# Low parts of the gate and up weights by adding transfers from HBM instead of VectorE subtractions

## The chip, the cores and the metric

The kernel runs on one core of a Trainium2 chip. A core has five engines with an instruction queue each: TensorE (PE in the profile, with its weight loads as PEld), VectorE (DVE), ScalarE (ACT), GpSimd (POOL) and SyncE (SP), and 16 DMA engines that move data between HBM and the on-chip memory. An engine works through its queue in order and waits for the others at semaphores. The metric is the device time of one execution in microseconds; of several runs the median is taken.

## The reference

A small decoder trunk on 512 tokens of width 1024: one short-convolution layer, then one sliding-window attention layer, each followed by a SwiGLU feed-forward block. All is float32.

```python
def swiglu(h, w_gate_up, w_down):
    g, u = jnp.split(h @ w_gate_up, 2, axis=-1)
    return (jax.nn.silu(g) * u) @ w_down

h = x
for l in range(DEPTH):                      
    if l < N_A:                             
        mix = short_conv_mixer(rmsnorm(h, a_pre_norm[l]), a_w_in[l], a_conv_w[l], a_w_out[l])
        h = h + rmsnorm(mix, a_post_norm[l])
    else:                                   
...
        h = h + rmsnorm(attn, b_post_norm[j])
    ff = swiglu(rmsnorm(h, ffn_pre_norm[l]), ffn_w_gate_up[l], ffn_w_down[l])
    h = h + rmsnorm(ff, ffn_post_norm[l])
return h
```

With D_FF = 2816 the gate and up projections have 22 column blocks of 128 each, in each of the two layers.

## The kernel before

**Two parts for each number.** TensorE multiplies in the type float32r, which holds fewer bits than float32. So every operand is kept as a rounded high part and the remainder, the low part. `mm3` (lines 167 to 170) multiplies with three matmuls: high weight by low activation (L168), high by high (L169), low weight by high activation (L170). In `project` the weights are the stationary operand: 8 blocks of 128 rows times three matmuls of 128x512 make 24 matmuls for one piece of weights, which is a 128x1024 tile of 512 KB and gives 128 output columns for all 512 tokens.

**How a piece is prepared.** `split_weights` (L150) takes four steps, on three engines:

- `fetch` (L132 to 138): SP issues a transfer of 512 KB from HBM into a buffer `raw`; the pool `wraw` has N_RAW = 6 of them. The next fetch into a buffer waits until its last reader is done.
- L161, L162: a pair `whi`, `wlo` is taken from the pool `wsp`, which has N_W = 5 of each. A pair comes free when TensorE has done with it.
- L163: ScalarE copies `raw` into `whi`, which rounds it (`AF.Copy`, no factor).
- L164: VectorE subtracts `whi` from `raw` into `wlo`.

`Ahead` (L317) does the same in two separate calls, L333 and L338, for the first three blocks of gate and up weights of a layer, written into an order by hand. `split_weights` with `slots=True` keeps its parts elsewhere (L157, L158).

**The feed-forward block.** `ffn` works in ROUNDS of blocks f: 0 to 5, 6 to 13, 14 to 21. For each f the gate piece and the up piece are prepared and projected (L731 to L737), and `gate_pair` or `gate` turns the two results into an activation: a sigmoid on ScalarE (L608 in `gate_pair`), multiplications on VectorE, rounding and remainder again. f = 0, 1 and 2 come from `Ahead`; f = 3 to 21 come from `split_weights`, 19 blocks with two pieces in each of the two layers, 76 pieces.

After the first two rounds `seven` multiplies that round's activations with the down weights by a scheme of seven products instead of eight. It uses the same five pairs `whi`, `wlo` (L669, L670) and the same six raw buffers, three jobs ahead (SEVEN_LEAD). One of its jobs is 12 matmuls, or 6 where it covers one block only, so that pairs come free there faster than in the projections. After the last round `first_half` and `second_half` multiply with the down weights directly and finish the layer.

**Order of the work.** Within a `tc.manual_schedule` block the instructions stand in each engine's queue as written. The projections of f = 3 to 21, the gates and `seven` are outside such blocks: there a scheduler picks the order at build time by its own estimates, and places the semaphore waits. At run time each engine keeps to that order.

GpSimd issues no transfer in this kernel. In the feed-forward blocks it only takes the power that ends a norm (L266, L286), at their end.

Of the kernel before, what the change touches and what calls it, by code (L numbers as in the profile page):

```python
# [10 lines left out]
F32 = mybir.dt.float32  # L11
F32R = mybir.dt.float32r
AF = mybir.ActivationFunctionType
ALU = mybir.AluOpType
# [41 lines left out]
def yoco_kernel(  # L56
# [20 lines left out]
    nc = tc.nc  # L77
# [14 lines left out]
    def name(s):  # L92
        uid[0] += 1
        return f"{s}_{uid[0]}"

    def slot(s, dt=F32, w=S):
        return big.tile([P, w], dt, tag="slot", name=name(s), padded_shape=[P, S])
# [10 lines left out]
    def bank(s, pool=None):  # L108

        if pool is None:  # L110
            pool = (ps_mm, ps_sc, ps_mm, ps_pt)[turn[0] % 4]
            turn[0] += 1
        return pool.tile([P, S], F32, tag="bank", name=name(s))
# [14 lines left out]
    def g(col, k):  # L128
        return gt[:, col + k : col + k + 1]


    def fetch(src, n=D):  # L132
        raw = wraw.tile([P, D], F32, tag="raw", name=name("raw"))
        dst = raw[:, :n]
        if len(src.shape) == 3:
            src, dst = src.rearrange("k p c -> p k c"), dst.rearrange("p (k c) -> p k c", c=S)
        nc.sync.dma_start(dst, src)
        return raw
# [8 lines left out]
            h = at[1].start // S  # L147
            return self.of[h][:, at[1].start - h * S : at[1].stop - h * S]

    def split_weights(src, raw=None, slots=False):  # L150
        if raw is None:
            raw = fetch(src)
        if slots:
            hi, lo = Two("whi", F32R), Two("wlo", F32R)
            for h in range(2):
                c = slice(h * S, (h + 1) * S)
                nc.scalar.activation(hi[:, c], raw[:, c], AF.Copy)  # L157
                nc.vector.tensor_tensor(out=lo[:, c], in0=raw[:, c], in1=hi[:, c].bitcast(F32),  # L158
                                        op=ALU.subtract)
            return hi, lo  # L160
        hi = wsp.tile([P, D], F32R, tag="whi", name=name("whi"))  # L161
        lo = wsp.tile([P, D], F32R, tag="wlo", name=name("wlo"))  # L162
        nc.scalar.activation(hi, raw, AF.Copy)  # L163
        nc.vector.tensor_tensor(out=lo, in0=raw, in1=hi.bitcast(F32), op=ALU.subtract)  # L164
        return hi, lo

    def mm3(out, whi, wlo, xhi, xlo, start, stop, **kw):
# [4 lines left out]
    def project(ps, w, x, c0=0, c1=S):  # L172

        whi, wlo = w
        for k in range(KT):
            kk = slice(k * P, (k + 1) * P)
            mm3(ps[:, c0:c1], whi[:, kk], wlo[:, kk], x[k][0][:, c0:c1], x[k][1][:, c0:c1],
                k == 0, k == KT - 1)
# [185 lines left out]
    with tc.manual_schedule(engines=ALL):  # L364
# [6 lines left out]
        for k in range(KT):  # L371
            hi, lo = xs[k]
            nc.scalar.activation(hi, xt[k], AF.Copy, scale=g(G_APRE, k))
            nc.vector.scalar_tensor_tensor(
                out=lo, in0=xt[k], scalar=g(G_APRE, k), in1=hi.bitcast(F32),
                op0=ALU.mult, op1=ALU.subtract,
            )
            for k0, k1 in CUTS:
                if k == max(k0 - 1, 0):
                    kk = slice(k0 * P, k1 * P)  # L380
                    for t in range(3):
                        hi, lo = ws[t]
                        nc.scalar.activation(hi[:, kk], first[t][:, kk], AF.Copy)
                        nc.vector.tensor_tensor(
                            out=lo[:, kk], in0=first[t][:, kk], in1=hi[:, kk].bitcast(F32),
                            op=ALU.subtract,
# [35 lines left out]
    for f in range(KT):  # L422
        if f < 2:
            pc, pu, pb = begun[f]
        else:
# [12 lines left out]
            out=t, in0=cu, scalar1=g(G_CONV, 16 + f), scalar2=None, op0=ALU.mult  # L438
        )
        for lag, tap in ((1, 1), (2, 0)):  # L440
            nc.vector.scalar_tensor_tensor(
                out=t[:, lag:], in0=cu[:, : S - lag], scalar=g(G_CONV, 8 * tap + f),
                in1=t[:, lag:], op0=ALU.mult, op1=ALU.add,
# [4 lines left out]
        hi, lo = slot("yhi", F32R), slot("ylo", F32R)  # L448
# [5 lines left out]
    def first_half(load, x, n, take, ws1=None):  # L454

        ws = [load(0, j) for j in range(n // 2)]
        raws = [fetch(load(1, j, True)) for j in range(min(2, n // 2))]
        ws1 = []

        def more():  # L460
            if len(ws1) < n // 2:
                ws1.append(split_weights(None, raws.pop(0), True))
                j = len(ws1) + len(raws)
                if j < n // 2:
                    raws.append(fetch(load(1, j, True)))

        with tc.manual_schedule(engines=ALL):
            pss = [bank("pmix") for _ in range(2)]
            for t in range(2):
                unit(pss[t], t, ws, x, range(n - 2), n)  # L470
                more()
            for t in range(2):
                unit(pss[t], t, ws, x, range(n - 2, n), n)
                take(t, 0, pss[t])
            for t in (2, 3):
                ps = bank("pmix")
                unit(ps, t, ws, x, range(n), n)
                more()
                take(t, 0, ps)
        return ws1  # L480
# [23 lines left out]
    def second_half(ws, x, n, res, ahead):  # L504

        k0 = n - 2
        for t in range(NB):
            ps = bank("pmix", ps_mm)
            if t == NB - 1:
                unit(ps, t, ws, x, range(k0), n)  # L510
                for b in range(4):
                    res.turn(b, (0, 1))
                unit(ps, t, ws, x, range(k0, n), n)
                for f in range(4):
                    res.split(0, f, 0)
            else:
                unit(ps, t, ws, x, range(n), n)
            if t == 0:
                ahead.one()
                ahead.one()  # L520
            res.take(t, 1, ps)
            if t < NB - 1:
                tile_done(res, t, ahead)
# [41 lines left out]
    def first_weights(l):  # L565
        return [w_gu[l, f, j] for f in range(3) for j in range(2)]
# [13 lines left out]
    ahead = Ahead(first_weights(0))  # L580
# [4 lines left out]
    def ffn(l, before, ahead, gain, gpres, following):  # L585
# [143 lines left out]
        for rd, (f0, f1) in enumerate(ROUNDS):  # L729
            final = rd == len(ROUNDS) - 1  # L730
            for f in range(2 if rd == 0 else f0, f1):  # L731
                pss = []
                for j in range(2):
                    w = ahead.ready[4 + j] if f == 2 else split_weights(w_gu[l, f, j])
                    pss.append(bank("pgu", (ps_sc, ps_pt)[j] if f == 2 else None))
                    project(pss[-1], w, xs)
                (gate if final else gate_pair)(*pss)  # L737
            n = f1 - f0
            if not final:
                seven(range(f0 // 2, f1 // 2), acts, rd == 0)  # L740
                acts = []
                continue

            def load(half, j, raw=False):
                src = w_dn[l, f0 // 2 + j, half : 4 - half : 3 - 2 * half]
                return src if raw else split_weights(src)

            res = Update(mix, gain, gpres, True)
            res.load()

            def take_last(t, half, ps):
                res.take(t, half, ps)
                res.scale(t, half)

            ws1 = first_half(load, acts, n, take_last)
            if gpres:
                ahead = Ahead(following)
                with tc.manual_schedule(engines=ALL):
                    second_half(ws1, acts, n, res, ahead)
                return res, ahead  # L760
            with tc.manual_schedule(engines=ALL):
                for t in range(NB):
                    if t < NB - 1:
                        ps = bank("pmix")
                        unit(ps, t, ws1, acts, range(n), n)
                        res.take(t, 1, ps)
                        res.mean(t)
                    else:
                        for c in (0, 256):
                            ps = bank("pmix")  # L770
                            unit(ps[:, :256], t, ws1, acts, range(n), n, 0, c, c + 256)
                            res.take_quarter(t, c, ps)
                    res.scale(t, 1)
                    for c in range(0, D, D if t < NB - 1 else S):
                        e = c + (D if t < NB - 1 else S)
                        res.update(t, c, e)
                        (nc.sync if c == 0 else nc.scalar).dma_start(out[t, :, c:e],
                                                                     hs[t][:, c:e])

    res, ahead = ffn(0, res, ahead, B_FFN[0], [G_KV, G_BPRE], [  # L780
        w_k[0], w_k[1], w_v[:, 0:D], w_v[:, D:], w_q[0], w_q[1]])
    xkv, xq = res.x
# [203 lines left out]
    with tc.manual_schedule(engines=ALL):  # L986
# [45 lines left out]
        src = [p.rearrange("p (h d) -> p h d", d=HD) for p in pv]  # L1032
        for j in range(NB):
            nc.scalar.activation(dst[j][0], src[j], AF.Copy)
        for j in range(NB):
            nc.vector.tensor_tensor(out=dst[j][1], in0=src[j], in1=dst[j][0].bitcast(F32),
                                    op=ALU.subtract)

    with tc.manual_schedule(engines=ALL):
        for i in range(KT + 2):  # L1040
            for c in ORDER.split():
# [5 lines left out]
                op, n = c[0], [int(d) for d in c[1:].rstrip("-")]  # L1047
                t = i - late
                if op == "g":

                    u = 2 * (t - EARLY - 1) + n[0]
                    if u in (-2, -1, 2, 3):
                        j = u + 2 if u < 0 else u
# [8 lines left out]
                elif op == "G":  # L1062
                    t += LEAD + 1
                    of = qs
                    if KT <= t < KT + 4:
                        j = t - KT
# [9 lines left out]
        ahead = Ahead(first_weights(1))  # L1076
# [10 lines left out]
        for t in range(NB):  # L1087
# [17 lines left out]
            if t < NB - 1:  # L1105
                tile_done(res, t)
    ffn(1, res, ahead, B_FFN[1], [], [])


# [85 lines left out]
```

## Time and profile before

| | |
|---|---|
| time, median of 3 runs | 1075.13 us (1073.75 to 1075.42) |
| the profiled execution | 1075.27 us |
| its span, first to last instruction | 1073.5 us |
| granted TensorE clock | 0.998 |
| HBM read, written | 103.46 MB, 2.10 MB |

The span is 1.8 us below the time of its execution. Busy time is what an engine spent in instructions, with waits left out. In the rows of instruction groups the line of kernel.py comes first, then engine, operation, output and inputs by their names, the count, the total busy time and the mean of one in ns; behind the second bar stands how long the engine was idle before them, and what ended most of that. The profile's chain is followed back from the last instruction, at each step to what released it.

### The profile page before, as it was taken

To read this page: it belongs to the slowest core of one execution; us is meant where nothing else is said; L and a number is where in the kernel's file an instruction comes from. 1 tells how busy PE (TensorE), PEld (TensorE's weight loads), DVE (VectorE), ACT (ScalarE), POOL (GpSimd) and SP (SyncE) were. 2 spreads that over 40 slices of the span, in tenths; PEclk is the share of its full clock that TensorE was granted. 3 is DMA by queue.
4 is the path that set the end of the run, shared out by engine and by line. 5 is a ranking of instruction groups with operands and counts; after the bars stand their busy time and mean duration, and the time that the engine had idled before them with its cause. 6 is when DMAs were issued, how large, how long until landed. Compare 5 with 4: busy or idle time off the path is not lost.

```text
span 1073.5 us, 13531 instructions
## 1 busy us (share of the span) xinstructions
PE 1060.8 (99%) x5268; PEld 894.0 (83%) x5268; DVE 656.5 (61%) x1069; ACT 444.6 (41%) x787; POOL 91.7 (9%) x90
## 2 busy tenths in 40 slices
PE   9899999999999999999999999999999999999997
PEld 7788888988888888888898888889888888888886
DVE  6665654376644784444568998666674568634344
ACT  6222234454433343223474777655353334322221
POOL 2421100000000000000021532020000000000001
PEclk9999999999999999999999999999999999999999
DMA  8433242030733044324212122302135221622201
GB/s 318 159 117 99 87 141 87 21 108 6 240 99 98 20 138 156 98 99 137 79 43 76 40 80 79 113 26 72 56 125 178 86 74 40 198 98 98 98 1 79
DMA packets 36864, 106.43 MB, mean 99 GB/s; under 512 B 3776, under 2 KB 4672, under 8 KB 36800
## 3 DMA queue, kind: packets, MB, share of 16 engines
q1 hardware_dynamic: 36224, 104.91, 30.3%
q8 instruction: 41, 0.67, 0.3%
q10 hardware_dynamic: 576, 0.66, 0.2%
q14 instruction: 23, 0.19, 0.1%
HBM read 103.46 MB, written 2.10 MB: 98 GB/s over the span
## 4 chain that ended last, share of the span: by engine, by line
PE 93%; DVE 3%; issue 1%; ACT 1%; POOL 1%; DMA 0%; POOLq 0%; DVEq 0%; SPq 0%; ACTq 0%
PE pgu L168 15%; PE pgu L169 15%; PE pgu L170 15%; PE pmix L169 4%; PE pmix L168 4%; PE pmix L170 4%; PE px L170 2%; PE px L169 2%; PE px L168 2%; PE pcub L392 2%; PE pz L170 1%; PE pz L169 1%; PE pz L168 1%; PE psc L867 1%; PE pq L168 1%
## 5 line engine op out<-in xcount | busy, mean ns | idle before, releaser
L168 PE MATMUL pgu<-xlo,whi 128*128 128x512 f32 (+1 forms) x768 | 285.6, 372 | 1.0 <-DVE xlo L312 1.0
L169 PE MATMUL pgu<-xhi,whi 128*128 128x512 f32 (+1 forms) x768 | 285.2, 371 | 0.0
L170 PE MATMUL pgu<-xhi,wlo 128*128 128x512 f32 (+1 forms) x768 | 285.1, 371 | 0.0
L163 ACT ACTIVATE whi<-raw 128x1024 fp32r<-128x1024 f32 x117 | 123.4, 1060 | 299.1 <-issue 159.4
L164 DVE TENSOR_TENSOR wlo<-raw,whi 128x1024 fp32r<-128x1024 f32 x117 | 156.1, 1335 | 123.2 <-ACT whi L163 123.2
L168 PEld LDWEIGHTS pgu<-xlo,whi 128*128 128x128 f32 x768 | 144.7, 188 | 26.4 <-DVE xlo L312 1.4
L169 PEld LDWEIGHTS pgu<-xhi,whi 128*128 128x128 f32 x768 | 144.7, 188 | 25.0
L170 PEld LDWEIGHTS pgu<-xhi,wlo 128*128 128x128 f32 x768 | 144.6, 188 | 24.8
L669 ACT ACTIVATE whi<-raw 128x1024 fp32r<-128x1024 f32 (+1 forms) x56 | 53.5, 955 | 99.9 <-PE pgu L169 32.9
L266 POOL TENSOR_TENSOR ur<-uv,mhalf 128x1 f32<-128x1 f32 x15 | 11.5, 770 | 757.6 <-DVE uv L262 757.6
L670 DVE TENSOR_TENSOR wlo<-raw,whi 128x1024 fp32r<-128x1024 f32 (+1 forms) x56 | 60.8, 1089 | 23.1 <-ACT whi L669 23.0
L168 PE MATMUL pmix<-wlo,ahi 128*128 128x512 f32 (+1 forms) x136 | 51.3, 377 | 0.0
L169 PE MATMUL pmix<-whi,ahi 128*128 128x512 f32 (+1 forms) x136 | 51.2, 377 | 0.0
L170 PE MATMUL pmix<-whi,alo 128*128 128x512 f32 (+1 forms) x136 | 51.2, 377 | 0.0
L610 DVE TENSOR_TENSOR gr<-pgu,gr 128x512 f32<-128x512 f32 x28 | 19.2, 690 | 49.2 <-PE pgu L170 49.2
L312 DVE SCALAR_TENSOR_TENSOR xlo<-xt,gt,xhi 128x256 fp32r<-128x256 f32 x64 | 27.0, 478 | 18.4 <-ACT xhi L311 18.1
L593 DVE TENSOR_TENSOR gate<-pgu,gate 128x512 f32<-128x512 f32 x16 | 11.1, 692 | 43.3 <-PE pgu L170 43.3
L665 DVE TENSOR_TENSOR raw<-raw,raw 128x1024 f32<-128x1024 f32 (+1 forms) x32 | 34.8, 1088 | 3.1 <-DMA raw<-in_w_dn_dram 2.7
L338 DVE TENSOR_TENSOR wlo<-raw,whi 128x1024 fp32r<-128x1024 f32 x18 | 21.8, 1224 | 18.8 <-ACT whi L333 18.4
L168 PE MATMUL px<-wlo,ahi 128*128 128x512 f32 x84 | 32.7, 389 | 0.0
L169 PE MATMUL px<-whi,ahi 128*128 128x512 f32 x84 | 32.7, 389 | 0.0
L170 PE MATMUL px<-whi,alo 128*128 128x512 f32 x84 | 32.7, 389 | 0.0
(238 smaller groups left out, 2031.3 us busy)
## 6 DMA issues: line engine op xcount, KB each, us to landing
raw<-in_w_gu_dram SPq DMA_DIRECT2D x88, 512.0 KB, 3.6
raw<-in_w_dn_dram SPq DMA_DIRECT2D x40, 512.0 KB, 3.4
raw<-in_w_in_dram SPq DMA_DIRECT2D x21, 512.0 KB, 4.5
raw<-in_w_out_dram SPq DMA_DIRECT2D x8, 512.0 KB, 3.5
raw<-in_w_q_dram SPq DMA_DIRECT2D x8, 512.0 KB, 3.6
raw<-in_w_o_dram SPq DMA_DIRECT2D x8, 512.0 KB, 3.5
xt<-in_xT_dram SPq DMA_DIRECT2D x8, 256.0 KB, 6.1
h<-in_x_dram SPq DMA_DIRECT2D x4, 512.0 KB, 5.8
```

Of the source, the lines that this page charges most:

```text
L163: nc.scalar.activation(hi, raw, AF.Copy)
L164: nc.vector.tensor_tensor(out=lo, in0=raw, in1=hi.bitcast(F32), op=ALU.subtract)
L168: nc.tensor.matmul(out, whi, xlo, start=start, stop=False, **kw)
L169: nc.tensor.matmul(out, whi, xhi, start=False, stop=False, **kw)
L170: nc.tensor.matmul(out, wlo, xhi, start=False, stop=stop, **kw)
L312: nc.vector.scalar_tensor_tensor(out=lo[:, c], in0=src, scalar=g(self.gpres[n], f), in1=hi[:, c].bitcast(F32), op0=ALU.mult, op1=ALU.subtract,
L338: nc.vector.tensor_tensor(out=lo, in0=raw, in1=hi.bitcast(F32), op=ALU.subtract)
L392: nc.tensor.matmul(ps, (whi, whi, wlo)[i][:, kk], (xhi, xlo, xhi)[i], start=k == i == 0, stop=k == KT - 1 and i == 2)
L610: nc.vector.tensor_tensor(out=gr, in0=pu, in1=gr, op=ALU.mult)
L665: nc.vector.tensor_tensor(out=w, in0=raw[other, c][:, :n], in1=w, op=ALU.subtract)
L669: nc.scalar.activation(hi[:, :n], w, AF.Copy)
L670: nc.vector.tensor_tensor(out=lo[:, :n], in0=w, in1=hi[:, :n].bitcast(F32), op=ALU.subtract)
```

## The change

Of the pieces f = 3 to 21 the low part is made in another way. ScalarE, which has rounded `raw` into `whi`, makes a second copy with the factor -1 into `wlo`. Then GpSimd issues a transfer of the same 512 KB from HBM that adds what it reads onto `wlo`, so that `wlo` holds raw - whi when it has landed. VectorE has no part in it. The fetch into `raw` by SP stays, since ScalarE rounds from there. All other splits are as before.

```diff
-    def split_weights(src, raw=None, slots=False):
+    def split_weights(src, raw=None, slots=False, add=False):
...
         hi = wsp.tile([P, D], F32R, tag="whi", name=name("whi"))
         lo = wsp.tile([P, D], F32R, tag="wlo", name=name("wlo"))
         nc.scalar.activation(hi, raw, AF.Copy)
-        nc.vector.tensor_tensor(out=lo, in0=raw, in1=hi.bitcast(F32), op=ALU.subtract)
+        if add:
+
+            nc.scalar.activation(lo, hi.bitcast(F32), AF.Copy, scale=-1.0)
+            nc.gpsimd.dma_start(lo, src, accum_op=ALU.add)
+        else:
+            nc.vector.tensor_tensor(out=lo, in0=raw, in1=hi.bitcast(F32), op=ALU.subtract)
         return hi, lo
...
                 for j in range(2):
-                    w = ahead.ready[4 + j] if f == 2 else split_weights(w_gu[l, f, j])
+                    w = ahead.ready[4 + j] if f == 2 else split_weights(w_gu[l, f, j], add=True)
```

## The prediction

> **What bounds the kernel now.** I read the page first, then what TensorE waits for, then the two feed-forward blocks stretch by stretch.
>
> ```profile
> span 1073.5 us, 13531 instructions
> ...
> PE 1060.8 (99%) x5268; PEld 894.0 (83%) x5268; DVE 656.5 (61%) x1069; ACT 444.6 (41%) x787; POOL 91.7 (9%) x90
> ...
> q1 hardware_dynamic: 36224, 104.91, 30.3%
> ...
> PE 93%; DVE 3%; issue 1%; ACT 1%; POOL 1%; DMA 0%; POOLq 0%; DVEq 0%; SPq 0%; ACTq 0%
> ...
> L163 ACT ACTIVATE whi<-raw 128x1024 fp32r<-128x1024 f32 x117 | 123.4, 1060 | 299.1 <-issue 159.4
> L164 DVE TENSOR_TENSOR wlo<-raw,whi 128x1024 fp32r<-128x1024 f32 x117 | 156.1, 1335 | 123.2 <-ACT whi L163 123.2
> ...
> L266 POOL TENSOR_TENSOR ur<-uv,mhalf 128x1 f32<-128x1 f32 x15 | 11.5, 770 | 757.6 <-DVE uv L262 757.6
> ...
> raw<-in_w_gu_dram SPq DMA_DIRECT2D x88, 512.0 KB, 3.6
> ```
>
> TensorE is busy in 1060.8 of 1073.5 us and holds 93% of the chain that ended last. VectorE, which the change relieves, holds 3%. The part of the kernel that changes is seen in the table by stretch (columns: stretch, its length, busy time and count of PE, PEld, DVE, ACT, POOL, clock, share of the DMA engines, GB/s). The six stretches are where the 76 changed pieces are multiplied: f 3 to 5, 6 to 13 and 14 to 21 of layer 0, then the same of layer 1.
>
> ```profile
> 226.00:258.60 32.60, 32.60 (x145) 26.99 (x144) 21.11 (x30) 9.54 (x15) 0.00 (x0) 1.00 0.17 49
> 287.10:374.10 87.00, 87.00 (x386) 72.03 (x385) 48.19 (x63) 28.13 (x40) 0.00 (x0) 1.00 0.28 86
> 412.10:499.20 87.10, 87.10 (x386) 72.11 (x385) 34.50 (x40) 24.51 (x32) 0.00 (x0) 1.00 0.33 110
> 749.60:782.10 32.50, 32.50 (x146) 26.90 (x145) 21.06 (x31) 9.44 (x15) 0.00 (x0) 1.00 0.19 55
> 810.50:897.60 87.10, 87.10 (x386) 72.16 (x385) 48.20 (x63) 28.24 (x40) 0.00 (x0) 1.00 0.27 86
> 935.60:1022.60 87.00, 87.00 (x386) 72.06 (x385) 34.41 (x40) 24.50 (x31) 0.00 (x0) 1.00 0.29 97
> ```
>
> TensorE is busy without a hole in all six, at full clock, so here there is no idle time to win back. One matmul starts every 87.0 / 386 = 0.225 us; a piece is 24 of them, 5.44 us (16 pieces in 87.1). POOL does nothing. The DMA engines are a third busy.
>
> **What goes.** 76 subtractions on VectorE (2 layers x 19 f x gate and up), 1.335 us each by the L164 row: 101 us. VectorE is on no path that TensorE waits for there, so this is worth 0. With it the raw buffer comes free about 1.2 us sooner, and SP may fetch the next piece so much earlier. Fetches are far ahead of need: worth 0 too.
>
> **What comes on ScalarE.** 76 negated copies, 128x1024. No row shows one; the nearest is the rounding copy of the same shape, 1.06 us (L163). In the long stretches ACT goes from 28.13 to 28.13 + 16 x 1.06 = 45 of 87 us, hidden by TensorE. The copy waits for the low buffer, whose last reader (L170) comes one matmul, 0.23 us, after that of the high one; behind it in ACT's queue stand the next rounding and the sigmoids, whose results TensorE needs one pair of pieces or more later. Hidden while that holds; uncovered it would cost 1.06 us a piece.
>
> **What comes on POOL and DMA.** 76 more transfers of 512 KB, issued by POOL behind ACT's negated copy; behind them in POOL's queue are only further ones (and L266 after the last). TensorE's first L170 of a piece now waits for the landing instead of for VectorE, and every later matmul queues behind it. Nothing in this trace is issued by POOL or adds on landing, so the cost is bounded by rows:
>
> - Issue on POOL: 0.77 us, from its smallest regular operation, L266; bounds 0 and 1.7 (its slowest row, quoted below).
> - Engine time of a transfer: q1 took 30.3% of 1073.5 = 325 us for 104.91 MB, that is 200 transfers of 0.524 MB: 1.63 us of all 16 engines. Landing takes 3.6 us, so 2.0 us of it is latency.
> - Engine time of an adding transfer: it must read what it adds to, besides the source. Low end: as a plain one, 1.63 us. High end: two whole landings without overlap, 7.2 us. I take two reads, 2 x 1.63 = 3.25 us, nearer to the row of the same size than to the end without overlap.
>
> The Trainium skill (Collectives: The Full Stack, Part 3, "Why ReduceScatter is half of AllGather") says that an add inside the DMA engine is free in itself, but that its two source reads halve the rate; no run here shows it yet. By that rule the engine time would also be 3.25 us, and by a rule where the read of the destination is free it would be 1.63.
>
> **Throughput.** In the fullest stretch plain transfers use 0.33 x 87.1 = 28.7 us; 16 x 3.25 = 52 us more make 81 of 87. It fits, at 93%, and saturates at (87.1 - 28.7) / 16 = 3.65 us a piece.
>
> **Latency.** In the middle of a stretch there are five buffers, four pieces x 5.44 = 21.8 us ahead of use: hidden. At the start of a stretch the buffers come from the seven-product stage (or the norm stage) and the lead is short. The timeline shows when ACT rounds the first changed piece, and when TensorE first reads its low part (columns: start, duration, instruction).
>
> ```profile
> 217.24 2.96 ACT L163 ACTIVATE whi<-raw 128x1024 fp32r<-128x1024 f32 x3
> 279.09 1.07 ACT L163 ACTIVATE whi<-raw 128x1024 fp32r<-128x1024 f32 x1 [0.73 <-PE px L170]
> 401.44 1.06 ACT L163 ACTIVATE whi<-raw 128x1024 fp32r<-128x1024 f32 x1 [1.61 <-PE px L170]
> 740.66 2.01 ACT L163 ACTIVATE whi<-raw 128x1024 fp32r<-128x1024 f32 x2
> 802.51 1.06 ACT L163 ACTIVATE whi<-raw 128x1024 fp32r<-128x1024 f32 x1 [0.72 <-PE px L170]
> 924.86 1.06 ACT L163 ACTIVATE whi<-raw 128x1024 fp32r<-128x1024 f32 x1 [1.61 <-PE px L170]
> ```
>
> ```profile
> 226.26 0.39 PE L170 MATMUL pgu<-xhi,wlo 128*128 128x512 f32 x1
> 287.46 0.39 PE L170 MATMUL pgu<-xhi,wlo 128*128 128x512 f32 x1
> 412.58 0.39 PE L170 MATMUL pgu<-xhi,wlo 128*128 128x512 f32 x1
> 749.68 0.39 PE L170 MATMUL pgu<-xhi,wlo 128*128 128x512 f32 x1
> 810.88 0.39 PE L170 MATMUL pgu<-xhi,wlo 128*128 128x512 f32 x1
> 936.00 0.39 PE L170 MATMUL pgu<-xhi,wlo 128*128 128x512 f32 x1
> ```
>
> After rounding and negating (2 x 1.06 = 2.12 us) there are left 6.9, 6.25, 9.0, 6.9, 6.25 and 9.0 us to issue, move and land. Just then SP refills its raw buffers, as the table of those six gaps shows; POOL's slowest row stands with it:
>
> ```profile
> 217.20:226.40 9.20, 9.20 (x42) 7.64 (x41) 9.18 (x16) 7.10 (x11) 0.00 (x0) 1.00 0.45 142
> 279.10:287.40 8.30, 8.30 (x38) 6.90 (x37) 6.34 (x8) 4.74 (x6) 0.00 (x0) 1.00 0.77 244
> 401.40:412.50 11.10, 11.10 (x51) 9.19 (x50) 7.57 (x10) 4.42 (x5) 0.00 (x0) 1.00 0.59 193
> 740.60:749.60 9.00, 9.00 (x41) 7.47 (x40) 8.89 (x15) 6.85 (x11) 0.00 (x0) 1.00 0.42 125
> 802.50:810.90 8.40, 8.40 (x39) 6.96 (x38) 6.57 (x9) 4.83 (x6) 0.00 (x0) 1.00 0.92 319
> 924.80:936.00 11.20, 11.20 (x52) 9.25 (x50) 7.67 (x10) 4.50 (x5) 0.00 (x0) 1.00 0.59 189
> ```
>
> ```profile
> L362 POOL TENSOR_TENSOR accx<-accx,sq 128x512 f32<-128x512 f32 x7 | 11.9, 1701 | 19.3 <-ACT sq L361 18.9
> ```
>
> I estimate that where both queues have packets they take turns, so that at a plain share s the adding transfer needs 3.25 / (1 - s/2): 4.2, 5.3, 4.6, 4.1, 6.0 and 4.6 us. With 0.77 for issue and 2.0 of latency that is 7.0, 8.05, 7.4, 6.9, 8.8 and 7.4 us. TensorE is late by 0.1, 1.8, 0 (1.6 to spare), 0, 2.5 and 0 us: 4.4 us in all. The second piece of a stretch has one piece time more and is on time if the first was. In the first gap ACT is busy 7.10 of 9.20 us already; four negated copies (4.2 us) run over its end by 2.1 us, and what they push back are copies for the seven-product stage, needed at 258: 0.
>
> **Sum.** The profiled execution took 1075.27 us, 1.8 more than its span and 0.14 over the median of the three runs. 1075.27 + 4.4 - 0.14 = 1079.5 us. With full sharing everywhere (6.5 us a transfer) the lateness would be 2.4, 3.0, 0.25, 2.4, 3.0, 0.25 = 11.3 us; with POOL at 1.7 us besides, 0.93 more at each, 16.9. So this case has a range of its own from 1077.3 to 1092.
>
> **The rivals.**
>
> - *Hidden* (27%). The adding transfer lands like a plain one: 0.77 + 3.6 = 4.4 us, under the shortest lead of 6.25. For it: nothing but TensorE is near its limit. Against it: 0.77 and 0.92 of the DMA engines are in use in two gaps. 1075 us, within 0.2%.
> - *The adding transfer becomes the bound* (23%). Above 3.65 us of engine time a stretch lasts as long as its transfers. Halfway to the high end, 5.4 us, the six stretches (plain share x length + pieces x 5.4 - length) grow by 5.3, 23.8, 28.0, 6.1, 22.8 and 24.6 us: 110.6, 1186 us. At 7.2 us: 1323. For it: at 3.25 only 7% is left in the fullest stretch. Against it: the two-read count stays below the limit.
> - *VectorE holds POOL up* (6%). In the conv stage, where POOL computes beside it, the L164 subtraction took up to 2.336 us, against 1.215 to 1.227 in layer 0's feed-forward block, where POOL rests:
>
> ```profile
> L164 DVE TENSOR_TENSOR wlo<-raw,whi x19: 1211/1226/2336, 41.6 to 141.0; 128x1024 fp32r<-128x1024 f32 x19
> ...
> L164 DVE TENSOR_TENSOR wlo<-raw,whi x42: 1215/1225/1227, 219.3 to 494.8; 128x1024 fp32r<-128x1024 f32 x42
> ```
>
>   If so each issue can wait for one VectorE operation, 1.22 us: lateness 1.3, 3.0, 0, 1.2, 3.7, 0 = 9.2, 1084 us. Against it: with the subtractions gone VectorE is idle in a third of these gaps or more, and POOL only issues. The Trainium skill (SBUF — State Buffer, "SBUF: two separate sides") says that POOL cannot write a transfer's descriptors while VectorE runs in a two-port fast mode; no run here shows descriptors written, and by that rule the time would be the same 1084, since the delay is one VectorE operation too.
> - *Faster* (4%). VectorE's reads would have to slow TensorE's, so that without them matmuls follow each other sooner: 2 ns less for the 76 x 24 = 1824 matmuls is 3.6 us, 1071.5; it decides from 1.2 ns on. Against it: in the stretches VectorE is busy 65%, 55% and 40%, and the spacing is 0.2248, 0.2254 and 0.2256 us.
>
> **How the numbers follow.** Late landings at the starts of stretches 40%, hidden 27%, transfer-bound 23%, POOL held up 6%, faster 4%. About 0.2%, 2.15 us, is what a measurement of this kernel tells from no change. So faster 4%, same 27%, slower 69%. The range runs from 1073 to 1170: it leaves out the faster case and the transfer-bound case above 5.2 us a transfer (a little over half of it, 13%), 17% together.
>
> **What would show it.** Six holes or fewer on TensorE, each ahead of the first L170 of pieces at f = 3, 6 and 14, put down to a DMA and 0 to 3 us long: the forecast. None: hidden. Holes throughout the second half of the stretches of 16 pieces, and a DMA share near 1: transfer-bound. On POOL, the issue's duration tells 0.77 from 1.7 or more; the packets' time of the new queue, over 76, tells 3.25 us from 1.63 and 7.2. HBM reads should rise by 76 x 0.524 = 39.8 MB, DVE's busy time fall by some 93 to 101 us and ACT's rise by 81. The forecast is wrong if the order of ACT's or POOL's work is changed so that a negated copy stands behind a wait for TensorE, or if an adding transfer's rows don't overlap.

## The result and the profile after

The changed kernel takes 1083.47 us (median of 12 runs, 1077.37 to 1087.31) against 1075.12 us before (12 runs, 1073.57 to 1075.68): ratio 1.0079, 95% interval 1.0061 to 1.0097, 8.3 us slower. 1079.5 us was forecast, with a range from 1073 to 1170. The runs spread five times as far as before. The execution that was profiled took 1081.08 us and is one of the better ones.

The page after, in the lines that answer to those shown of before:

```profile
span 1079.0 us, 13772 instructions
...
PE 1060.7 (98%) x5268; PEld 891.9 (83%) x5268; DVE 571.3 (53%) x993; ACT 517.1 (48%) x863; POOL 158.2 (15%) x166
...
q1 hardware_dynamic: 36224, 104.91, 29.2%
q0 software_dynamic: 10944, 39.85, 20.7%
...
PE 88%; DMA 4%; DVE 3%; issue 3%; ACT 1%; POOL 1%; POOLq 0%; DVEq 0%; SPq 0%; ACTq 0%
...
L167 POOL DMA_DIRECT2D wlo<-in_w_gu_dram x76 | 66.5, 875 | 495.8 <-ACT wlo L166 238.6
...
L166 ACT ACTIVATE wlo<-whi 128x1024 fp32r<-128x1024 f32 x76 | 79.8, 1053 | 0.7
...
raw<-in_w_gu_dram SPq DMA_DIRECT2D x88, 512.0 KB, 4.4
wlo<-in_w_gu_dram POOLq DMA_DIRECT2D x76, 512.0 KB, 7.9
```

The work has moved as written: VectorE is busy 85 us less, ScalarE 72 us more, POOL issues 76 transfers, and 39.85 MB come over a queue q0 that was not there. TensorE's busy time is the same to 0.1 us, so the loss is idle time of TensorE. (Busy time counts the overlap of neighbouring instructions once; by the durations of the single instructions the two engines changed by 92.5 and 80.0 us, as forecast.) The chain that ended last now has a share of DMA, 4%. One row of what TensorE waits for (total us, times, longest) is new:

```profile
PE pgu L175 <- DMA wlo<-in_w_gu_dram: 4.8, 3, 2.3
```

These lines of the kernel have moved by five: L173, L174 and L175 are the old L168, L169 and L170. L175 is the matmul that reads the low part. The timeline of TensorE shows where the two longest of these waits stand (start, duration, instruction, idle time and what ended it):

```profile
285.48 0.39 PE L173 MATMUL pgu<-xlo,whi 128*128 128x512 f32 x1
285.70 0.39 PE L174 MATMUL pgu<-xhi,whi 128*128 128x512 f32 x1
287.87 0.50 PE L175 MATMUL pgu<-xhi,wlo 128*128 128x512 f32 x1 [1.78 <-DMA wlo<-in_w_gu_dram]
...
812.29 0.39 PE L174 MATMUL pgu<-xhi,whi 128*128 128x512 f32 x1
815.03 0.50 PE L175 MATMUL pgu<-xhi,wlo 128*128 128x512 f32 x1 [2.35 <-DMA wlo<-in_w_gu_dram]
```

These are the first pieces of f = 6, in layer 0 and layer 1. Matmuls normally start 0.227 us apart; here the third starts 2.17 and 2.74 us after the second, so the holes are 1.94 and 2.51 us. By the same count there are smaller ones at the second piece of f = 6 in layer 0 (0.26) and at f = 14 in the two layers (0.25 and 0.79). Together 5.7 us. None stands later than the second piece of a stretch: in the four long stretches (columns as before) the length less the busy time of PE is 1.88, 0.09, 2.35 and 0.63 us, which is the idle time of these holes.

```profile
285.50:375.00 89.50, 87.62 (x386) 71.93 (x385) 33.59 (x50) 40.49 (x52) 11.43 (x14) 1.00 0.75 175
413.10:500.50 87.40, 87.31 (x386) 71.99 (x385) 20.63 (x28) 36.01 (x43) 11.24 (x13) 1.00 0.83 203
812.10:901.80 89.70, 87.35 (x386) 72.01 (x385) 33.59 (x50) 40.49 (x53) 11.42 (x14) 1.00 0.75 176
939.90:1027.80 87.90, 87.27 (x385) 71.95 (x384) 20.60 (x28) 36.02 (x43) 11.22 (x13) 1.00 0.79 190
```

Over a whole stretch the DMA engines are at 0.75 to 0.83, up from about 0.3, and not full. At its start they are. From the issue of the first adding transfer of f = 6 to its landing, in the two layers:

```profile
280.00:287.80 7.80, 6.09 (x27) 4.69 (x26) 1.37 (x2) 7.50 (x9) 2.81 (x4) 1.00 1.03 286
806.60:815.00 8.40, 6.08 (x27) 4.69 (x25) 1.37 (x2) 8.08 (x10) 3.42 (x4) 1.00 1.00 272
```

The share counts the packets that start in the window with their whole time, so it can come out a little above 1.

For a comparison that leaves out chance at the start and end of an execution I take the time from the first gate matmul of layer 0 to the first matmul of the last product. Before:

```profile
190.15 0.28 PE L168 MATMUL pgu<-xlo,whi 128*128 128x256 f32 x1
...
1022.58 0.39 PE L168 MATMUL pmix<-wlo,ahi 128*128 128x512 f32 x1
```

After:

```profile
188.38 0.28 PE L173 MATMUL pgu<-xlo,whi 128*128 128x256 f32 x1
...
1027.82 0.39 PE L173 MATMUL pmix<-wlo,ahi 128*128 128x512 f32 x1
```

That is 832.43 and 839.44 us, 7.0 us more; 5.7 are the holes, 1.0 lies in ten delays of about 0.1 us, in the matmuls right behind a hole and at the first pieces of f = 3, and the rest in smaller ones. This profiled execution came to the first gate matmul 1.8 us sooner than before's by chance (188.38 us here, 188.44 to 189.95 in the three further ones shown below), and its end is 0.3 us longer in the span and 0.3 outside it: 7.0 - 1.8 + 0.6 = 5.8 us, the difference of the two profiled executions. I call the first of these times the middle part below.

### The profile page after: what moved, and what is told of

Same layout as the page of the kernel before. It is cut to its first block, busy times and chain, and to the rows that moved or that the text cites. A ratio compares the mean times of both kernels' runs of the same rounds, so it can differ in the third digit from the quotient of the medians.

```text
span 1079.0 us, 13772 instructions
## 1 busy us (share of the span) xinstructions
PE 1060.7 (98%) x5268; PEld 891.9 (83%) x5268; DVE 571.3 (53%) x993; ACT 517.1 (48%) x863; POOL 158.2 (15%) x166
## 3 DMA queue, kind: packets, MB, share of 16 engines
q1 hardware_dynamic: 36224, 104.91, 29.2%
q0 software_dynamic: 10944, 39.85, 20.7%
## 4 chain that ended last, share of the span: by engine, by line
PE 88%; DMA 4%; DVE 3%; issue 3%; ACT 1%; POOL 1%; POOLq 0%; DVEq 0%; SPq 0%; ACTq 0%
PE pgu L175 15%; PE pgu L173 15%; PE pgu L174 15%; PE pmix L173 4%; PE pmix L175 4%; PE pmix L174 4%; DMA wlo<-in_w_gu_dram 3%; PE px L173 2%; PE px L174 2%; PE px L175 2%; PE pcub L397 2%; PE pz L174 1%; PE pz L173 1%; PE pz L175 1%; PE psc L872 1%
## 5 line engine op out<-in xcount | busy, mean ns | idle before, releaser
L175 PE MATMUL pgu<-xhi,wlo 128*128 128x512 f32 (+1 forms) x768 | 286.1, 373 | 4.9 <-DMA wlo<-in_w_gu_dram 4.8
L173 PE MATMUL pgu<-xlo,whi 128*128 128x512 f32 (+1 forms) x768 | 285.7, 372 | 1.0 <-DVE xlo L317 1.0
L174 PE MATMUL pgu<-xhi,whi 128*128 128x512 f32 (+1 forms) x768 | 285.3, 371 | 0.0
L175 PEld LDWEIGHTS pgu<-xhi,wlo 128*128 128x128 f32 x768 | 144.6, 188 | 32.8 <-DMA wlo<-in_w_gu_dram 8.0
L173 PEld LDWEIGHTS pgu<-xlo,whi 128*128 128x128 f32 x768 | 144.7, 188 | 26.0 <-DVE xlo L317 1.4
L174 PEld LDWEIGHTS pgu<-xhi,whi 128*128 128x128 f32 x768 | 144.7, 188 | 24.9
L167 POOL DMA_DIRECT2D wlo<-in_w_gu_dram x76 | 66.5, 875 | 495.8 <-ACT wlo L166 238.6
L166 ACT ACTIVATE wlo<-whi 128x1024 fp32r<-128x1024 f32 x76 | 79.8, 1053 | 0.7
L169 DVE TENSOR_TENSOR wlo<-raw,whi 128x1024 fp32r<-128x1024 f32 x41 | 63.0, 1541 | 24.4 <-ACT whi L163 24.4
L614 DVE TENSOR_TENSOR gr<-pgu,gr 128x512 f32<-128x512 f32 x28 | 19.1, 689 | 75.8 <-ACT gr L613 75.8
L173 PE MATMUL pmix<-wlo,ahi 128*128 128x512 f32 (+1 forms) x136 | 51.3, 377 | 0.0
L615 DVE TENSOR_TENSOR gr<-pgu,gr 128x512 f32<-128x512 f32 x28 | 19.2, 690 | 60.7 <-PE pgu L175 60.7
L174 PE MATMUL pmix<-whi,ahi 128*128 128x512 f32 (+1 forms) x136 | 51.2, 377 | 0.0
L175 PE MATMUL pmix<-whi,alo 128*128 128x512 f32 (+1 forms) x136 | 51.2, 377 | 0.0
L597 DVE TENSOR_TENSOR gate<-pgu,gate 128x512 f32<-128x512 f32 x16 | 11.0, 690 | 60.6 <-ACT gate L596 60.6
L598 DVE TENSOR_TENSOR gate<-pgu,gate 128x512 f32<-128x512 f32 x16 | 11.1, 692 | 51.8 <-PE pgu L175 51.8
```

The lines of the kernel that those rows point to most:

```text
L166: nc.scalar.activation(lo, hi.bitcast(F32), AF.Copy, scale=-1.0)
L167: nc.gpsimd.dma_start(lo, src, accum_op=ALU.add)
L173: nc.tensor.matmul(out, whi, xlo, start=start, stop=False, **kw)
L174: nc.tensor.matmul(out, whi, xhi, start=False, stop=False, **kw)
L175: nc.tensor.matmul(out, wlo, xhi, start=False, stop=stop, **kw)
```

## The experiments

Theory A: the loss is the late landing of the first piece or two of a stretch, made late by SP's own transfers of that moment. Theory B: every adding transfer, or every added copy, costs a little. Theory C: 16 transfers in a row are more than the DMA engines carry. Each ratio is to runs of the kernel before that were taken beside that kernel's own, so it need not be the quotient of the times shown.

| kernel | time, us | ratio to before, 95% | middle part, us, against 832.43 |
|---|---|---|---|
| changed kernel | 1083.47 | 1.0079 (1.0061 to 1.0097) | +7.0 |
| starts by VectorE | 1073.58 | 0.9995 (0.9987 to 1.0004) | +0.1 |
| only the starts | 1083.41 | 1.0080 (1.0067 to 1.0094) | +8.8 |
| copies only | 1075.12 | 1.0003 (0.9994 to 1.0012) | 0.0 |
| low part last | 1075.84 | 1.0008 (0.9999 to 1.0016) | +0.4 |
| transfer without the add | 1078.50 | 1.0036 (1.0024 to 1.0048) | 0.0 |
| half of the fetches | 1077.48 | 1.0027 (1.0016 to 1.0038) | +2.0 |
| six pairs | 1075.17 | 1.0012 (1.0003 to 1.0022) | +4.5 |

### The starts of the stretches by VectorE

```diff
-                    w = ahead.ready[4 + j] if f == 2 else split_weights(w_gu[l, f, j], add=True)
+                    w = ahead.ready[4 + j] if f == 2 else split_weights(w_gu[l, f, j], add=f not in (3, 6, 14))
```

> Blocks f = 3, 6 and 14 (12 of 76 pieces, the first two of each stretch) get their low part from VectorE again; the other 64 keep the adding transfer. Theory A (the loss is the late landing of the first piece of a stretch): the holes ahead of f = 3, 6 and 14 go, and the time is within 1.5 us of before, near 1075, with before's spread of about 2 us instead of 10. Theory B (each adding transfer or each added copy costs a little everywhere): 64/76 of the 8.3 us stays, 1082. Theory C (the 16 transfers of a stretch come too fast for the DMA engines): 14 of 16 stay, 1081 or more.

1073.58 us (1073.42 to 1075.54), no different from before, with before's spread. 64 of the 76 transfers are still there and TensorE waits for none of them. Theory B and theory C fall: the loss hangs on the first two pieces of a stretch.

### Only the starts by adding transfers

```diff
-                    w = ahead.ready[4 + j] if f == 2 else split_weights(w_gu[l, f, j], add=True)
+                    w = ahead.ready[4 + j] if f == 2 else split_weights(w_gu[l, f, j], add=f in (3, 6, 14))
```

> Only blocks f = 3, 6 and 14 (12 of 76 pieces) use the adding transfer, the rest VectorE. Theory A: the first landing of a stretch is as late as in the changed kernel, since nothing stands before it in its queue, so most of the loss stays, 1079 to 1083, with holes of about 2 to 2.5 us ahead of f = 6 in both layers. Theories B and C: 12/76 of 8.3 us, 1076.4.

1083.41 us (1082.44 to 1083.87, four runs): 12 of the 76 pieces make a loss as large as that of all 76, though not with quite the same holes. TensorE's wait for them:

```profile
PE pgu L175 <- DMA wlo<-in_w_gu_dram: 6.1, 3, 2.6
```

The holes stand at f = 3 and f = 6 of layer 0 (1.58 and 2.30 us) and f = 6 of layer 1 (2.73). The hole at f = 3 had been missing in the changed kernel; why it is here the runs do not show. The trace shows something more. Near its start every execution but one of those profiled has a stretch of 3.4 us or more at half clock, that of before too; here there is a second one, behind the hole at f = 6:

```profile
292.30:295.70 3.40, 3.40 (x10) 2.66 (x9) 0.00 (x0) 0.00 (x0) 0.00 (x0) 0.50 1.01 378
```

### The negated copies alone

```diff
-            nc.gpsimd.dma_start(lo, src, accum_op=ALU.add)
+            nc.vector.tensor_tensor(out=lo, in0=raw, in1=hi.bitcast(F32), op=ALU.subtract)
```

> All 76 pieces get the negated copy on ScalarE, and VectorE then writes the low part over it; no transfer is issued by GpSimd. It leaves the adding transfer out and prices the copy alone. Theory A: 0, 1075, since the chain grows by 1.06 us and the shortest lead is 6 us. A theory that ScalarE's longer queue makes pieces or gates late: several us, up to the whole 8.3.

1075.12 us, and the middle part is 832.46 us. ScalarE's 76 copies are hidden, as forecast.

### The low part read last

In `project` (all its calls):

```diff
         for k in range(KT):
             kk = slice(k * P, (k + 1) * P)
-            mm3(ps[:, c0:c1], whi[:, kk], wlo[:, kk], x[k][0][:, c0:c1], x[k][1][:, c0:c1],
-                k == 0, k == KT - 1)
+            nc.tensor.matmul(ps[:, c0:c1], whi[:, kk], x[k][1][:, c0:c1], start=k == 0, stop=False)
+            nc.tensor.matmul(ps[:, c0:c1], whi[:, kk], x[k][0][:, c0:c1], start=False, stop=False)
+        for k in range(KT):
+            kk = slice(k * P, (k + 1) * P)
+            nc.tensor.matmul(ps[:, c0:c1], wlo[:, kk], x[k][0][:, c0:c1], start=False, stop=k == KT - 1)
```

> The changed kernel, but a projection multiplies with the high part for all eight row blocks first (16 matmuls) and with the low part last (8), so the low part is needed 14 matmuls later, 3.2 us. Theory A: holes of 1.9 and 2.5 us go, and 1.9 to 2.5 us more lateness in a bad run would just be covered: 1075 to 1077. Theory B and C: no change from 1083.

1075.84 us (1073.96 to 1076.34). All 76 transfers are there and take as much engine time (20.6% on q0); the first low part is read 3.2 us later, and of TensorE's waits for them one is left:

```profile
PE pgu L186 <- DMA wlo<-in_w_gu_dram: 0.2, 1, 0.2
```

So lateness at the start is the loss. One start of this execution was 3.5 us late, the 3.2 us that are covered and a hole of 0.34 us. The change can be had for next to nothing this way; it wins nothing either, since TensorE had no idle time there.

### The transfer without the add

```diff
-            nc.gpsimd.dma_start(lo, src, accum_op=ALU.add)
+            nc.gpsimd.dma_start(lo, src)
```

> The transfer that GpSimd issues writes the weights over the negated copy instead of adding them: it leaves the addition out, and its low part is the whole weight. It prices the add. Theory A: engine time falls from 2.9 us a transfer to about 1.6 and the landing in a start from 8 us to about 6.5, so the loss falls from 8.3 to 0 to 4 us, 1075 to 1079. If the issue by GpSimd and its latency are what is late, and not the add, 1082 as before.

It leaves the addition out. The queue and the landings on its page, and the issues with their shortest, median and longest duration in ns:

```profile
q0 software_dynamic: 10944, 39.85, 12.4%
...
wlo<-in_w_gu_dram POOLq DMA_DIRECT2D x76, 512.0 KB, 4.6
...
L167 POOL DMA_DIRECT2D wlo<-in_w_gu_dram x76: 540/540/755, 219.1 to 996.8; - x76
```

Engine time is 12.4% x 1074.5 / 76 = 1.75 us a transfer, with the add 20.7% x 1079.0 / 76 = 2.94; the median landing is 4.6 instead of 7.9 us. In the middle part no loss is left (832.44 us). What is late is thus the add and not the issue by POOL as such. The issue gets 0.33 us shorter too (0.54 for 0.87 us in the median), a tenth of what the landing gains. That the add costs a second read fits the engine time, 1.7 times that without it, but is not shown apart. At f = 6 the first landings take 5.70 and 5.34 us from issue, with 5.9 us to go until TensorE reads them, so even this transfer is on time by only 0.2 and 0.6 us. The time is still 1078.50, at the upper end of what was expected, and that is no hole: in the profiled execution of this kernel (1076.63 us, the fastest of the five) the engines wait at the end, 3.5 us from the landing of the last output to the end of the span, where the changed kernel has 1.4. What is waited for there the trace does not tell, so that part stays open.

### Half of SP's fetches

```diff
-            raw = fetch(src)
+            raw = fetch(src[:, :S], S) if add else fetch(src)
...
-        nc.scalar.activation(hi, raw, AF.Copy)
         if add:
-
+            nc.scalar.activation(hi[:, :S], raw[:, :S], AF.Copy)
+            nc.scalar.activation(hi[:, S:], raw[:, :S], AF.Copy)
```

The adding transfer makes the low part whatever the high part lacks, so the two still add up to the weight, as far as the low part can hold it.

> The 76 fetches by SP into raw take only the first half of each piece (256 KB), and ScalarE rounds that half into both halves of the high part: it leaves out the second half of the high parts. The adding transfer stays whole. It halves what competes with it at a start. Theory A with contention: the landing ahead of f = 6 gets 1 to 2.5 us sooner, and the time 1075 to 1079. Without contention (the landing is late by its own length alone): 1082 as before.

1077.48 us (1075.83 to 1078.20). The landings come sooner, though the adding transfers are the same:

```profile
wlo<-in_w_gu_dram POOLq DMA_DIRECT2D x76, 512.0 KB, 6.2
raw<-in_w_gu_dram SPq DMA_DIRECT2D x76, 256.0 KB, 2.8
```

At f = 6 the first landings take 5.41 and 5.16 us from issue, for 7.81 and 8.38 in the changed kernel, and the issue stands as far ahead of the read as there (5.8 and 5.9 us). The holes ahead of f = 6 and 14 are gone in both layers. Two others came, 0.42 and 1.29 us, ahead of f = 3, where SP fetches down weights in whole pieces and ScalarE has two operations for one; that hole of 1.29 us is most of the 2.0 us that the middle part has lost here. So what competes at f = 6 is SP's refilling of raw buffers. This supports the contention in theory A; what makes f = 3 late here was not taken apart.

### Six pairs

```diff
-N_SLOT, N_WIDE, N_RAW, N_W = 46, 8, 6, 5
+N_SLOT, N_WIDE, N_RAW, N_W = 42, 8, 6, 6
```

> Six pairs of high and low weight tiles instead of five, paid for with four activation tiles less (42 for 46). The first changed piece of a stretch can be begun one job of the seven-product stage sooner, 2.7 us (1.4 where jobs are short). Theory A: most of the holes of 1.9 and 2.5 us go, 1075 to 1078. If throughput is short: little change, 1081 to 1083. If four activation tiles less make the gates wait, it is slower, with TensorE waiting for others than the transfers.

1075.17 us (1073.31 to 1078.54). The holes ahead of f = 6 shrink to 1.35 and 1.41 us and do not go. The time falls further than they do, in the execution that was profiled, because the stage before the middle part is shorter with six pairs (its first gate matmul starts at 185.0 us, 3.4 us sooner than in the changed kernel, in part because a half-clock window early in the execution is missing there), while the attention stage between the blocks takes 1.4 us longer with fewer activation tiles. The expectation had the sign right and the reason only in part.

### The changed kernel again, three times

No edit.

> The changed kernel once more, for a second draw of its holes. Open: why its runs spread over 10 us (1077.4 to 1087.3) where before spreads over 2. Theory A1: a hole of about 2 us or more ahead of f = 3, 6 or 14 sometimes makes the clock gate give half speed for 3.41 us, which costs 1.7 us each time; then a run over 1083 shows one or more such stretches in its clock, and its holes sum to its excess less 1.7 us for each. Theory A2: the clock stays, and the holes alone are longer in slow runs; then they sum to the whole excess.

> The changed kernel, a third draw; as again1: by A1 a run over 1083 shows half-clock stretches of 3.41 us behind its holes, by A2 longer holes alone.

> The changed kernel, a fourth draw; as again1: by A1 a run over 1083 shows half-clock stretches of 3.41 us behind its holes, by A2 longer holes alone.

They took 1086.67, 1085.14 and 1083.74 us. The first, behind its holes at f = 6, in windows of the clock:

```profile
287.30:290.60 3.30, 0.55 (x3) 0.30 (x2) 0.00 (x0) 3.27 (x4) 0.87 (x1) 1.00 1.05 283
290.60:294.00 3.40, 3.40 (x9) 2.67 (x8) 0.00 (x0) 0.16 (x1) 0.87 (x1) 0.50 1.05 275
294.00:297.40 3.40, 3.40 (x16) 2.76 (x15) 0.00 (x0) 0.39 (x1) 0.00 (x0) 1.00 1.05 273
816.30:819.70 3.40, 1.55 (x7) 1.29 (x8) 0.00 (x0) 2.99 (x4) 0.95 (x2) 1.00 1.07 301
819.70:823.10 3.40, 3.40 (x10) 2.66 (x9) 0.00 (x0) 0.00 (x0) 0.79 (x1) 0.50 1.05 276
```

TensorE idles, and then runs a window of 3.4 us at a granted clock of 0.50: 9 or 10 matmuls where the next window has 16. All four draws:

| draw | time, us | middle part | holes at f = 6, layers 0 and 1 | at f = 14 | at f = 3 | half-clock windows in the middle part |
|---|---|---|---|---|---|---|
| profile after | 1081.08 | +7.0 | 1.94, 2.51 | 0.25, 0.79 | 0, 0 | 0 |
| again1 | 1086.67 | +11.0 | 2.92, 2.22 | 0, 1.64 | 0, 0 | 2 |
| again2 | 1085.14 | +9.8 | 2.85, 3.08 | 0, 1.03 | 0.23, 0 | 1 |
| again3 | 1083.74 | +9.6 | 3.38, 2.83 | 0.45, 0 | 0.45, 0 | 1 |

The middle part less the holes is 1.3 to 1.5 us in the draw without a half-clock window, 2.5 to 2.6 in those with one and 4.2 in that with two: 1.2 to 1.5 us a window by this subtraction. Counted directly it is 1.6 us in every one of them: matmuls start 0.427 us apart there instead of 0.227, eight times or so. That is near the 1.7 expected; what the subtraction lacks are the short delays, which are 0.6 to 0.8 us in these three draws and 1.0 in the first. A1 holds. Of A2 one half does: the holes differ by 2 us from draw to draw, but the clock does not stay, and adds to them.

## Why the prediction was right, and where its size was off

**TensorE bounds, and VectorE's work is worth nothing.** Right. 85 us less of it moved nothing; starts by VectorE, which drops 64 of 76 subtractions, is level with before. The rival *faster* is out: matmuls in a stretch start 0.227 us apart before and after.

**The copies are hidden.** Right, 0 us by copies only.

**Engine time of an adding transfer, 3.25 us from two reads.** Nearly right: 2.94 us. Against the same queue without the add it is 1.7 times, against SP's plain fetches (29.2% x 1079.0 / 200 = 1.57 us) 1.9 times. The Trainium skill (Collectives: The Full Stack, Part 3) gives a measured 1.93 between the rates of AllGather and ReduceScatter, and puts it down to the two reads of the latter. The 1.9 here agrees with that, the 1.7 in the same queue is lower.

**Issue, 0.77 us.** 0.875 us by the L167 row. The rival of VectorE holding POOL up finds nothing: the issues take 0.86 to 1.05 us each. That its 1084 us is the figure nearest to the measured one is chance.

**Throughput fits.** Right: 0.83 in the fullest stretch, forecast as 0.93. The rival of the transfers as the bound is out, and theory C with it.

**The lead at the starts decides, at f = 6.** Right in the place and the mechanism; the rival *hidden* is out. The sizes of the profiled execution, 1.94 and 2.51 us for 1.8 and 2.5 forecast, are luck in part: over four executions of the kernel (the draws above) the holes have means of 2.8 us in layer 0 and 2.7 in layer 1, so the order of the two, which came from the plain shares 0.77 and 0.92, does not hold.

**At f = 3, no lateness to speak of.** Right by two errors that cancel. The landings take 5.4 to 6.2 us from issue, where 7.0 and 6.9 had been worked out. But the negated copies stand behind other work of ScalarE and end 6.1 and 5.8 us ahead of the read in the two layers, instead of 6.9. (At f = 6 and 14 these leads came as they had been read, 6.2 and 9.0 us.)

**The size of the sum.** 4.4 us were forecast and 8.3 came. The mis-sized terms are these, by the four draws:

- The lateness at f = 6 was forecast from one plain share. The eight holes there have a mean of 2.7 us, 5.4 us for the two layers instead of 4.3. The landings take 7.8 to 9.3 us from issue, for 8.05 and 8.8 forecast.
- At f = 14 the sum said 1.6 us to spare, and the holes come to 1.0 us for both layers in the mean. This term has the largest error: 7.4 us were forecast for issue, latency and moving, and the landings take 7.7 to 9.6 us, as long as at f = 6, though the plain share before was 0.59 there. In layer 1 the issue also starts 0.96 us behind the copy instead of 0.3, for a reason that the trace does not show. So 3.25 / (1 - s/2) with the plain share of before is the step that was mis-sized. One thing that it left out is on record: up to the landing of a first transfer at f = 6 or 14 the new queue moved 1.3 to 1.7 pieces, not one, so the transfers behind it had part of the DMA engines, which were at 0.88 to 1.03.
- "The second piece is on time if the first was" is not a full answer, since the first was not: there is a hole of 0.26 us at it in the profiled execution.
- The half clock behind a long hole was not in the sum at all: one window a draw on average, 1.6 us. That is also why the runs spread, with the varying holes.
- The short delays, 0.6 to 1.0 us, and in the profiled execution the longer end, 0.6 us, had been set to zero.

The upper end of the case's own range, 1092, had been worked out from full sharing and a slower issue, and every run is under it. As a bound for each start it does not hold: it allowed 0.25 us at f = 14 with full sharing and 1.2 with the slower issue, where 1.64 came, and 2.4 us or more at f = 3, where at most 0.45 came.

## What to carry to other kernels

A transfer that takes over work from an engine off the critical path is worth nothing where the bound engine has no idle time, and its longer latency is paid where the lead is shortest: look at the first use after a stage change, not at the steady stretch. There, compare the lead with the landing beside whatever the other queues move just then. If the lead is short by a few us, reading the late operand last in the consumer's order can be cheaper than more buffers.

## What the hardware showed that was not expected

The clock went to half after holes far shorter than the window it was halved for. In the records of the granted clock all these half-clock windows began a whole number of windows of 3.413 us after the last change of the clock (74 and 154 in again1, 229 in again2, 75 in again3 and in only the starts). Where 1.89 to 2.92 us of a hole lay inside one such window, the next was at half clock: five cases. Where a hole of 2.51 to 2.85 us was split so that neither side had more than 1.81 us, it was not: four cases. One hole with 1.94 us in one window had no such consequence, so in this measure a limit, if there is a sharp one, lies near 1.9 us; no run was made to fix it. The Trainium skill (TensorE: Matmul & The Clock Gate, Part 1) gives half rate after at least one idle window of about 3.4 us; by the runs here, which decide for this kernel, 1.89 us, somewhat more than half a window, was enough.
